# Eight weight rests of an encoder's second MLP: an adding transfer in place of a VectorE subtraction

## The chip, the cores and the metric

The kernel runs on one core of a Trainium2 chip. The metric is the device time of one execution in microseconds (us); the median over runs is compared. Engines are named as the profile names them: PE is the matrix engine (PEld its weight loads), DVE is VectorE, ACT is ScalarE, POOL is GpSimd, SP is SyncE, which issues most of the DMA transfers. SBUF is the on-chip memory with 128 partitions, PSUM the accumulator memory of PE.

## The reference

An encoder of two layers over 256 tokens of width 1024, all in float32. The first half of a layer is a token mixer (pooling, dilated attention, gates). The change lies in the second half, the gated MLP:

```python
def _conv_ffn(xn, w_up, conv_w, conv_b, w_down):
    a, gval = jnp.split(xn @ w_up, 2, axis=-1)
    a = lax.conv_general_dilated(a, ...) + conv_b
    return (jax.nn.gelu(a) * gval) @ w_down

for layer in range(DEPTH):
    h = h + _token_mixer(_rmsnorm(h, norm1[layer]), ...)
    h = h + _conv_ffn(_rmsnorm(h, norm2[layer]), w_up[layer], ...)
return _rmsnorm(h, norm_f)
```

Here w_up is 1024 x 5632 and w_down 2816 x 1024 for each layer.

## The kernel before, in words

**Two parts of every number.** PE multiplies in the type float32r, which keeps fewer bits than float32. So every operand stands as a sum of two parts: the first part is the value rounded to float32r, the rest is what rounding took away. A product is then made of three matmuls: first x first, first x rest, rest x first. For weights, ScalarE makes the first part (the tile wh, a cast, line 191) and VectorE the rest (the tile wl, the loaded weights minus the first part, line 192). Both lines stand in `Weights.open_next`.

**Loads and pieces.** The class `Weights` (line 87) holds the whole program of weight loads in order. SyncE brings 1 MB at a time into one of three buffers (`RAW = 3`, tile raw, line 126), so that each load reuses the buffer of the third load before it. A load holds two pieces, each [128 partitions, 2, 512]; a piece is cast and subtracted into one of five pairs of buffers (`BUFS = 5`, tiles wh and wl). `get` hands out the next piece and prepares pieces ahead: in the MLP's up-projection four of them (`W.LOOK + 1`, line 1485). With five buffers that means: when PE begins with a piece, the buffer of the one before it comes free, and into that goes the piece which is needed four pieces later. `_split` (line 149) first issues the loads that have become due, then the cast and the subtraction.

**The up-projection.** The order of the MLP's work is written out in `ORDER` (line 40): "a0 g0 v0 a1 g1 a2 g2 a3 g3 a4 g4 r5 d0 d1 d2 d3 d4". An "a" or "g" is a sum of 256 rows x 512 columns of the activated branch or of the gate, "r5" the rest of both, "d" parts of the down-projection; v0 belongs to the first layer only. A sum takes two loads (the loop over j in lines 303 to 320) and so four pieces. `by_rows` (line 671) gets a piece, makes its 12 matmuls (`v_sum`, line 661: six for each of two halves of the rows, the second of the six being the first that reads the rest), frees the piece, and calls `unit` (line 1452).

**What else goes on.** After a sum VectorE turns its rows out of PSUM in blocks (line 701). After a "g" sum, `cross` (line 684) sends the turned rows of the pair in 16 transfers of 64 KB to their places; four of them are issued by SyncE in each `unit` of the next "a" sum (line 691). They stand in the same in-order queue as the weight loads. From the unit numbers in `TWOS` (line 42) on, `two_up` (line 1384) makes the convolution, gelu and gate of two blocks of channels, in four steps over four units, on ScalarE and VectorE (lines 1392 to 1430).

**The order of instructions.** `keep_order` (line 643) keeps PE, ScalarE and VectorE to the order of the source from the first up-projection to the last down-projection piece. SyncE's and GpSimd's instructions are placed by the scheduler of the framework, each queue being run in order. GpSimd does only small sums for the norms (lines 467 to 472) once the tables have been built at the start.

Of the kernel before, what the change touches and what calls it, by code (L numbers as in the profile page):

```python
# [10 lines left out]
F32 = mybir.dt.float32  # L11
F32R = mybir.dt.float32r
AF = mybir.ActivationFunctionType
ALU = mybir.AluOpType
# [72 lines left out]
class Weights:  # L87
# [8 lines left out]
    def __init__(self, tc, pool, idle):  # L96
        self.tc, self.nc, self.pool, self.idle = tc, tc.nc, pool, idle
        self.loads, self.pieces = [], []
        self.n_loaded, self.n_split, self.n_got = 0, 0, 0
        self.raw, self.split = {}, {}  # L100
        self.live = set()
        self.behind, self.n_behind = (), 0
        self.n_scaled, self.gains = 0, None
        self.due = 0

    def add(self, src, shape, cuts, tag=None):

        n = len(self.loads)
        self.loads.append((src, shape, tag))
        return [(n, cut, c_shape) for cut, c_shape in cuts]  # L110
# [59 lines left out]
    def open_next(self):  # L170


        nc, i = self.nc, self.n_split
        n, cut, shape, slot = self.pieces[i]
        if slot is None:
            self.live.add(i)
            h, l = (
                self.pool.tile([P, *shape], F32R, tag=tag, bufs=self.BUFS, name=f"{tag}{i}")
                for tag in ("wh", "wl")
            )  # L180
        else:
            tag, part, of = (*slot, 0, 1)[:3]
            if part == 0:
                self.shared = self.idle.tile([P, of, 2, *shape], F32R, tag=tag, name=f"{tag}{i}")
            h, l = self.shared[:, part, 0], self.shared[:, part, 1]
        src = cut(self.raw[n])
        self.split[i] = (h, l)
        self.n_split += 1
        if i >= self.n_scaled:
            return [(  # L190
                lambda: nc.scalar.copy(out=h, in_=src),  # L191
                lambda: nc.vector.tensor_sub(out=l, in0=src, in1=h.bitcast(F32)),  # L192
            )]

        def scaled(j):
            k = i // 2 * shape[0] + j
            g = self.gains[:, k : k + 1]
            return (
                lambda: nc.scalar.activation(h[:, j], src[:, j], AF.Copy, scale=g),
                lambda: nc.vector.scalar_tensor_tensor(  # L200
                    out=l[:, j], in0=src[:, j], scalar=g, in1=h[:, j].bitcast(F32),
                    op0=ALU.mult, op1=ALU.subtract,
                ),
            )

        return [scaled(j) for j in range(shape[0])]
# [15 lines left out]
def encoder(ctx, tc, x, w_in, w_pool, pool_scale, w_a, w_b, w_o, norm1, norm2, w_up, conv_w,  # L222
            conv_b, w_down, rel_bias, norm_f, onehot, edges, out):
    nc = tc.nc
# [9 lines left out]
    W = Weights(tc, wpool, big)  # L234

    def cols(w, c0):

        src = w[:, c0 : c0 + 256].rearrange("(k p) c -> p k c", p=P)
        return W.add(
            src, (8, 256), [((lambda t, j=j: t[:, :, j * P : (j + 1) * P]), (8, P)) for j in (0, 1)]  # L240
        )

    def rows(w, r0, n=2, c0=0, width=1024, tag=None, pieces=2):

        src = w[r0 : r0 + n * P, c0 : c0 + width].rearrange("(k p) c -> p k c", p=P)
        h = n // pieces
        return W.add(
            src, (n, width), [((lambda t, j=j: t[:, j * h : (j + 1) * h, :]), (h, width)) for j in range(pieces)],
            tag,
        )  # L250

    for l in range(DEPTH):
        if l == 0:
            slots = (("m2", 0, 2), ("m2", 1, 2), ("ybig",), ("at2",))
            for j in range(2):
                kept = rows(w_in[l], j * 512, 4, C_V, 512)
                more = rows(w_in[l], j * 512, 4, C_V + 512, 512, "k1" if j else None)
                for n in range(2):
                    W.use(kept[n : n + 1], slots[2 * j + n : 2 * j + n + 1])
                    W.use(more[n : n + 1])  # L260
            W.n_scaled = len(W.pieces)
        else:
            W.use(rows(w_in[l], 512, 4, C_V, 512), (("ybig",), ("at2",)))
            for j in range(2):
                W.use(rows(w_in[l], j * 512, 4, C_V + 512, 512))

        def half_of(w, c0, half, n):
            for j in range(n):
                W.use(rows(w, j * 512, 4, c0 + half.start, 512))

        for half in HALVES:
            half_of(w_in[l], 0, half, 2)
        for c0 in (C_Q + 512, C_K + 512, C_Q + 1024, C_K + 1024):
            half_of(w_in[l], c0, HALVES[0], 2)
        for c in PAIRS:
            q = cols(w_in[l], C_Q + c * 256)
            k = cols(w_in[l], C_K + c * 256)
            if c == 0:
                pool = W.add(
                    w_pool[l].rearrange("g (k p) c -> p (g k) c", p=P), (8, 256),  # L280
                    [((lambda t, j=j: t[:, 4 * j : 4 * j + 4, :]), (4, 256)) for j in range(2)],
                )
                q.insert(1, pool[0])
                k.insert(1, pool[1])
            W.use(q + k)
        half_of(w_in[l], C_V + 1024, HALVES[0], 2)

        for half in HALVES:
            half_of(w_in[l], C_GP, half, 2)
        for half in HALVES:  # L290
            half_of(w_a[l], 0, half, 2)
            half_of(w_in[l], C_GA, half, 2)
            half_of(w_b[l], 0, half, 1)
        for c in range(4):
            W.use(rows(w_o[l], c * 256))
        slots = (("v1",), ("ybig",), ("at2",))
        for kind, n in ORDER.split():
            n = int(n)
            if kind == "v":
                if l + 1 < DEPTH:  # L300
                    W.use(rows(w_in[l + 1], 0, 4, C_V, 512), (("m2", 0, 2), ("m2", 1, 2)))
                continue
            for j in range(2):
                if kind == "d":
                    W.use(rows(w_down[l], (4 * n + 2 * j) * P))
                elif kind == "r":
                    src = w_up[l][j * 512 : (j + 1) * 512].rearrange("(k p) c -> p k c", p=P)
                    c0 = (4 * n * P, 4 * n * P + DFF)
                    W.use(
                        W.add(  # L310
                            tuple(src[:, :, c : c + 256] for c in c0), (4, 2, 256),
                            [
                                ((lambda t, j=j: t[:, 2 * j : 2 * j + 2].rearrange("p k h c -> p k (h c)")), (2, 512))
                                for j in (0, 1)
                            ],
                        )
                    )
                else:
                    p = rows(w_up[l], j * 512, 4, (kind == "g") * DFF + 4 * n * P, 512)
                    W.use(p, slots[2 * j : 2 * j + 2] if (kind, n) == ("a", 0) else ())  # L320
        W.use(rows(w_down[l], (NF - 2) * P))


    h = const.tile([P, 2, D], F32, name="h")
# [214 lines left out]
    def proj(x2):  # L539

        i, (wh, wl) = W.get()
        flush()
        ps = mmp.tile([P, 2, S], F32, tag="mm", name="proj_ps")
        two_sums(ps, lambda k: wh[:, k, :], lambda k: wl[:, k, :], x2, KD)
        W.free(i)
        return ps[:, 0], ps[:, 1]

    def halves(a):

        return a.rearrange("p (t m) -> p t m", t=2)  # L550
# [352 lines left out]
    for l in range(DEPTH):  # L903
# [296 lines left out]
        for c in PAIRS:  # L1200
            for n in range(4):
                src, rest = (halves(a) for a in proj(x2))
# [115 lines left out]
        def begin_mlp():  # L1318
# [12 lines left out]
            out=way[:, 0].rearrange("p j c r -> p c j r"),  # L1331
            in_=th[0][:, 1].rearrange("p (c j r) -> p c j r", c=4, j=4),
# [4 lines left out]
        for j in range(4):  # L1337
            nc.sync.dma_start(
                out=way[32 * j : 32 * j + 32, 1].rearrange("x i c r -> x i (c r)"), in_=blocks_of[j]
# [125 lines left out]
        for kind, n in ORDER.split():  # L1465
# [20 lines left out]
            n = int(n)  # L1486
# [39 lines left out]
```

## Time and profile before

| what | value |
|---|---|
| median of 3 runs (lowest, highest) | 857.34 us (857.09, 857.48) |
| profiled execution: span | 856.1 us |
| second layer's up-projection in it, g0 to r5 | 681.1 to 789.9 us |
| its subtractions for the rests on DVE, whole kernel (line 192) | 278 subtractions, 336.9 us busy |
| its casts on ACT, whole kernel (line 191) | 278 casts, 288.9 us busy |
| mean granted clock of PE | 0.999 |

The profile is one execution. A row of the view by groups gives the line, the engine, what is written and read, the shape, how many, then busy time and the mean of one, then how long the engine was idle just before such instructions and what ended that idling. A row of the timeline gives start and length in us from the span's start. A DMA row gives the queue that issued it (SPq for SyncE's, POOLq for GpSimd's), how many, their size and the median time from issue to landing. Idle time of an engine that does not set the end costs nothing.

### The profile page before, as it was taken

The numbers are of one execution on the slowest core, as the hardware profiler recorded it, in microseconds if no ns is written. First come the engines' busy times: TensorE is split into PE (matmuls) and PEld (weight loads), VectorE is DVE, ScalarE is ACT, GpSimd is POOL, SyncE is SP. The second block draws the span as 40 slices with busy tenths as digits, with TensorE's granted clock in tenths as the row PEclk, the third lists the DMA queues.
The fourth block names the chain that finished last, engine by engine and source line by source line (L and its number), as shares of the span: only waits on it lengthen the run. The fifth ranks groups of instructions, "written<-read, shape, count | busy, mean of one in ns | idle before, by whom it ended". The sixth has DMA issues, their size and how long they took to land.

```text
span 856.1 us, 11279 instructions
## 1 busy us (share of the span) xinstructions
PE 849.1 (99%) x4030; PEld 713.0 (83%) x4030; DVE 648.8 (76%) x918; ACT 476.9 (56%) x700; POOL 19.9 (2%) x53
## 2 busy tenths in 40 slices
PE   9999999999999999999999999999999999999997
PEld 7888888888888888888888889888888888888886
DVE  6967898566767788999656597986568658999874
ACT  7735475444545566767444445654445436766762
POOL 1120000000010000000000000000000000000001
PEclk9999999999999999999999999999999999999999
DMA  8787684764947777777626676758559376777751
GB/s 313 243 256 247 190 278 149 220 231 127 315 173 233 225 236 241 249 232 257 220 99 210 226 233 192 237 162 247 199 200 310 112 228 190 244 242 242 255 181 50
DMA packets 101340, 186.07 MB, mean 217 GB/s; under 512 B 9806, under 2 KB 28702, under 8 KB 101284
## 3 DMA queue, kind: packets, MB, share of 16 engines
q1 hardware_dynamic: 100484, 183.62, 64.9%
q0 software_dynamic: 496, 1.33, 0.5%
q8 instruction: 32, 0.52, 0.3%
q10 hardware_dynamic: 304, 0.40, 0.1%
q14 instruction: 24, 0.20, 0.1%
HBM read 160.65 MB, written 1.59 MB: 190 GB/s over the span
## 4 chain that ended last, share of the span: by engine, by line
PE 99%; POOLq 0%; DVE 0%; ACT 0%; issue 0%; DVEq 0%; POOL 0%; ACTq 0%
PE rows_ps L666 61%; PE res_ps L563 6%; PE res_ps L565 6%; PE res_ps L564 6%; PE v_ps L666 5%; PE proj_ps L535 3%; PE v_ps L788 3%; PE proj_ps L537 2%; PE s_ps L1076 1%; PE o_ps L1151 1%; PE s_ps L1071 1%; PE o_ps L1147 1%; PE xt_ps L494 1%; PE pool_ps L529 0%; PE pool_ps L527 0%; PE pool_ps L528 0%
## 5 line engine op out<-in xcount | busy, mean ns | idle before, releaser
L192 DVE TENSOR_TENSOR wl<-raw,wh 128x1024 fp32r<-128x1024 f32 x278 | 336.9, 1218 | 145.4 <-ACT wh L191 141.6
L666 PE MATMUL rows_ps<-wh,x 128*128 128x512 f32 x1344 | 420.1, 391 | 0.0
L191 ACT CAST wh<-raw 128x1024 fp32r<-128x1024 f32 x278 | 288.9, 1049 | 212.7 <-PE rows_ps L666 131.0
L666 PEld LDWEIGHTS rows_ps<-wh,x 128*128 128x128 f32 x1344 | 252.4, 188 | 52.2
L666 PE MATMUL rows_ps<-wl,x 128*128 128x512 f32 x672 | 261.6, 389 | 0.0
L666 PEld LDWEIGHTS rows_ps<-wl,x 128*128 128x128 f32 x672 | 126.2, 188 | 25.6
L563 PE MATMUL res_ps<-wh,actq 128*128 128x512 f32 (+1 forms) x152 | 57.5, 378 | 0.0
L564 PE MATMUL res_ps<-wl,actq 128*128 128x512 f32 (+1 forms) x152 | 57.4, 378 | 0.0
L565 PE MATMUL res_ps<-wh,actk 128*128 128x512 f32 (+1 forms) x152 | 57.4, 378 | 0.0
L666 PE MATMUL rows_ps<-wh,po 128*128 128x512 f32 x128 | 41.2, 393 | 0.0
L564 PEld LDWEIGHTS res_ps<-wl,actq 128*128 128x128 f32 x152 | 28.6, 188 | 5.4
L563 PEld LDWEIGHTS res_ps<-wh,actq 128*128 128x128 f32 x152 | 28.6, 188 | 5.4
L565 PEld LDWEIGHTS res_ps<-wh,actk 128*128 128x128 f32 x152 | 28.6, 188 | 5.3
L535 PE MATMUL proj_ps<-x,wh 128*128 128x512 f32 x128 | 32.2, 393 | 0.0
L701 DVE STREAM_TRANSPOSE up_rows<-rows_ps 128x512 f32<-128x512 f32 x40 | 26.3, 693 | 3.1 <-PE rows_ps L666 3.1
L666 PEld LDWEIGHTS rows_ps<-wh,po 128*128 128x128 f32 x128 | 24.0, 188 | 4.9
L1393 ACT ACTIVATE yg<-a,prm 128x256 f32<-128x256 f32 x44 | 26.5, 602 | 1.4
L563 PE MATMUL res_ps<-wh,m 128*128 128x512 f32 (+1 forms) x72 | 26.7, 371 | 0.0
L535 PEld LDWEIGHTS proj_ps<-x,wh 128*128 128x128 f32 x128 | 23.1, 189 | 4.2
L565 PE MATMUL res_ps<-wh,m 128*128 128x512 f32 (+1 forms) x72 | 26.4, 366 | 0.0
L564 PE MATMUL res_ps<-wl,m 128*128 128x512 f32 (+1 forms) x72 | 26.4, 366 | 0.0
L463 ACT ACTIVATE junk<-h 128x512 f32<-128x512 f32 (+1 forms) x19 | 10.5, 552 | 27.5 <-DVE h L461 27.5
(225 smaller groups left out, 1051.6 us busy)
## 6 DMA issues: line engine op xcount, KB each, us to landing
raw<-in_w_in_dram SPq DMA_DIRECT2D x56, 1024.0 KB, 5.5
raw<-in_w_up_dram SPq DMA_DIRECT2D x40, 1024.0 KB, 6.0
raw<-in_w_down_dram SPq DMA_DIRECT2D x22, 1024.0 KB, 5.8
up_turned<-up_rows SPq DMA_DIRECT2D x160, 64.0 KB, 3.9
raw<-in_w_a_dram SPq DMA_DIRECT2D x8, 1024.0 KB, 5.0
raw<-in_w_o_dram SPq DMA_DIRECT2D x8, 1024.0 KB, 5.1
qk<-qk_rows SPq DMA_DIRECT2D x64, 64.0 KB, 2.7
pt<-rows SPq DMA_DIRECT2D x64, 64.0 KB, 3.6
```

The costliest lines, as they stand in the source:

```text
L191: lambda: nc.scalar.copy(out=h, in_=src),
L192: lambda: nc.vector.tensor_sub(out=l, in0=src, in1=h.bitcast(F32)),
L463: nc.scalar.activation(junk, new, AF.Square, scale=D**-0.5, accum_out=ss[:, n : n + 1])
L535: nc.tensor.matmul(ps, wh(k), x2[:, k], start=(k == 0), stop=False)
L537: nc.tensor.matmul(ps[:, 1], wl(k), x2[:, k, 0], start=False, stop=(k == nk - 1))
L563: nc.tensor.matmul(ps, ah, wh, start=first, stop=False)
L564: nc.tensor.matmul(ps, ah, wl, start=False, stop=False)
L565: nc.tensor.matmul(ps, al, wh, start=False, stop=last)
L666: nc.tensor.matmul(ps, x2[:, 2 * n + j, part, t, :], w[:, j, :], start=(n + m == 0), stop=(n == of - 1 and m == 5),)
L701: nc.vector.transpose(out=out[:, :, t].rearrange("p j c r -> p c j r"), in_=ps[t].rearrange("p (c j r) -> p c j r", c=4, j=4),)
L788: return nc.tensor.matmul(ps[g][t], a[:, k, t, :], w[:, k % 2, :], start=k == 0 and kind == "hh", stop=k == KD - 1 and kind == "hl",)
L1393: nc.scalar.activation(y, aj, AF.Identity, bias=b, scale=w1)
```

## The change

In the second layer, for the sums a1 to a4 and g1 to g4 (not a0 and g0), the second piece of the second load is marked: one piece in four, eight in all. For a marked piece ScalarE makes the first part as before and then writes its negative into the tile of the rest; a transfer from GpSimd's queue then adds the loaded weights to that tile. VectorE has nothing to do for it. The result is the same sum, the loaded weights minus the first part.

```diff
@@ class Weights, __init__
         self.due = 0
+        self.summed = set()
@@ open_next
         src = cut(self.raw[n])
         self.split[i] = (h, l)
         self.n_split += 1
+        if i in self.summed:
+            return [(
+                lambda: nc.scalar.copy(out=h, in_=src),
+                lambda: nc.scalar.mul(out=l, in_=h.bitcast(F32), mul=-1.0),
+                lambda: nc.gpsimd.dma_start(out=l, in_=src, accum_op=ALU.add),
+            )]
         if i >= self.n_scaled:
             return [(
                 lambda: nc.scalar.copy(out=h, in_=src),
@@ encoder, the loop over ORDER
                     p = rows(w_up[l], j * 512, 4, (kind == "g") * DFF + 4 * n * P, 512)
+                    if l and j and n:
+                        W.summed.add(len(W.pieces) + 1)
                     W.use(p, slots[2 * j : 2 * j + 2] if (kind, n) == ("a", 0) else ())
```

## Prediction

> **What bounds the kernel now.** I read the busy time of the page first, then what the matrix engine waits for, then the stage of the change by itself.
>
> ```profile
> PE 849.1 (99%) x4030; PEld 713.0 (83%) x4030; DVE 648.8 (76%) x918; ACT 476.9 (56%) x700; POOL 19.9 (2%) x53
> ...
> PE gain_ps L377 <- DVE mhalf L366: 1.0, 1, 1.0
> ...
> 681.10:789.90 108.80, 108.80 (x481) 90.10 (x481) 89.80 (x126) 67.76 (x93) 0.00 (x0) 1.00 0.72 236
> 789.90:856.10 66.20, 60.22 (x278) 50.18 (x277) 47.12 (x70) 36.02 (x57) 2.16 (x7) 0.98 0.46 160
> ...
> 681.09 108.80 PE rows_ps L666 x480
> ```
>
> The second line is all that the view of waits has for PE: one wait of 1.0 us in the whole span. The next two are the view by stretches: length, then the busy time of PE, weight loads, DVE, ACT and POOL, the granted clock, the DMA share, GB/s. From 681.1 to 789.9 us, the up-projection of the second layer, PE is busy for all of its 108.80 us at a granted clock of 1.00. The last line, from the chain of waits, says that this is the path: 480 matmuls back to back, 0.2267 us each, so 12 matmuls or 2.72 us for a weight piece, four pieces or 10.88 us for a sum. VectorE's 89.80 us lie beside that. So VectorE's work here ends no wait of PE; the only question is whether the pieces still arrive in time.
>
> How they arrive now:
>
> ```profile
> L192 DVE TENSOR_TENSOR wl<-raw,wh 128x1024 fp32r<-128x1024 f32 x32 | 38.9, 1214 | 16.0 <-ACT wh L191 14.5 <-DMA up_turned<-up_rows 1.5
> L191 ACT CAST wh<-raw 128x1024 fp32r<-128x1024 f32 x33 | 34.6, 1049 | 25.9 <-PE rows_ps L666 18.3 <-DMA raw<-in_w_up_dram 7.5
> L1427 ACT ACTIVATE actq<-yg 128x512 fp32r<-128x512 f32 x6 | 3.8, 630 | 2.1 <-DVE yg L1419 2.1
> ...
> 689.28 1.05 ACT L191 CAST wh<-raw 128x1024 fp32r<-128x1024 f32 x1 [1.67 <-PE rows_ps L666]
> 690.37 1.22 DVE L192 TENSOR_TENSOR wl<-raw,wh 128x1024 fp32r<-128x1024 f32 x1 [1.50 <-ACT wh L191]
> 755.05 1.03 ACT L191 CAST wh<-raw 128x1024 fp32r<-128x1024 f32 x1
> ...
> 843.20 0.22 POOL L467 TENSOR_SCALAR ss<-ss 128x1 f32<-128x1 f32 x1 [171.95 <-ACT junk L463]
> ```
>
> The first three rows are groups of the stretch from 690 to 780 us (busy us, mean ns, idle before), the others single instructions, the last of them GpSimd's first one after the stage. The cast of a piece starts when PE lets go of the buffer of the piece five before it, and that piece is used four pieces later. The cast at 689.28 is that of the first piece the change touches (a1's fourth); the sum g0 begins at 681.09, seven pieces ahead of it, so PE comes to it at 681.09 + 7 x 2.72 = 700.13, and to its rest one matmul later, at 700.36. Its rest is there at 690.37 + 1.22 = 691.59, 8.8 us early. The cast of a4's fourth piece, at 755.05, is the latest against its use, which comes at 765.64 with the rest: 10.6 us, where the first has 11.1.
>
> **The change part by part.** *VectorE.* Eight subtractions leave, 8 x 1.214 = 9.7 us of VectorE's time. What hides them already is PE's 108.80 us, so the gain on the path is nothing.
>
> *ScalarE.* Eight negations come, 1024 elements each from SBUF to SBUF. There is no such row; the cast of the same shape takes 1.05 us, and twice the 512-element multiplication of L1427 takes 1.26. I take 1.06 us, since the cast is the same shape. They are 8.5 us beside ACT's 67.76 of 108.80. Where ACT only casts, each falls into the 1.67 us that ACT waits for PE before the next cast. Where activations follow (after the last six), it moves the next cast by up to 1.1 us, and plain pieces are 8.8 us early. So zero, as long as pieces are early by more than a microsecond.
>
> *GpSimd.* Its queue waits for each negation. The stretch has no GpSimd work at all (0.00 in its column), and the norm's sums start at 843.20, over 50 us after the stage, so nothing waits behind it on that queue.
>
> *The transfer* is the open cost. It carries 512 KB from one SBUF tile into another, adds, and its landing releases both PE (for the rest) and SyncE (for the buffer of the loaded weights). The trace has no adding transfer. Its nearest rows:
>
> ```profile
> fd<-fsb POOLq DMA_DIRECT2D x2, 4.0 KB, 4.0
> bt<-fd POOLq DMA_DIRECT2D x5, 256.0 KB, 5.7
> DMA to landing us min/median/max: 5.1/5.7/6.7
> ...
> raw<-in_w_up_dram SPq DMA_DIRECT2D x12, 1024.0 KB, 6.3
> up_turned<-up_rows SPq DMA_DIRECT2D x64, 64.0 KB, 3.8
> ```
>
> The last number of a row is the median time from issue to landing; the third line gives the spread of the five bt transfers, the last two are of the stretch from 690 to 780 us. A transfer from GpSimd's queue takes 4.0 us when it carries next to nothing. Bytes cost, by SyncE's rows, 6.3 - 3.8 = 2.5 us for 960 KB more, so 1.3 us for 512 KB. To add, the engines must fetch the old values as well, 1 MB in all, hence about 2.6 us. Ends: 4.0 + 1.3 = 5.3 us if the second operand is free. By GpSimd's own rows 252 KB cost 1.7 us, so 1 MB costs 6.9: 10.9 us. I take 4.0 + 2.6 = 6.6, and 0.2 more because the DMA engines are already 0.72 busy in this stage and some of the transfers will share with a load: A = 6.8 us, an estimate. It sits nearer to SyncE's rows because they are the same long runs in this very stage, while the bt rows are five transfers on their way at once.
>
> The Trainium skill ("DMA: Bandwidth & Descriptors", section "Anatomy of one DMA — SWDGE (gpsimd) path") gives for such a transfer about 2.0 us plus bytes over 436 GB/s, an estimate of 3.2 us for 512 KB, with which nothing below would be late and the time would stay at 857.3. The rows do not agree: by that rule 256 KB would take 2.6 us where bt shows 5.7, and 4 KB 2.0 where fd shows 4.0.
>
> *First deadline: the rest itself.* From the start of the cast: 1.05 cast, 1.06 negation, about 0.1 for the two hand-overs, 2.2 us, then A. There are 11.1 us (10.6 for the latest), so by itself this holds until A = 8.9 (8.4). At 6.8 it has 2.1 us left.
>
> *Second deadline: the buffer of the loaded weights.* This is the tight one. There are three such buffers: each load reuses that of the third load before it, and SyncE waits at that load with the row transfers of the up-projection queued behind it.
>
> ```profile
> 691.62 0.37 SPq L126 DMA_DIRECT2D raw<-in_w_up_dram  x1
> 692.85 7.51 SPq L691 DMA_DIRECT2D up_turned<-up_rows  x12
> 700.46 1.00 SPq L126 DMA_DIRECT2D raw<-in_w_up_dram  x1
> ...
> 718.95 0.53 SPq L126 DMA_DIRECT2D raw<-in_w_up_dram  x1
> 719.52 5.80 SPq L691 DMA_DIRECT2D up_turned<-up_rows  x8
> 725.42 0.54 SPq L126 DMA_DIRECT2D raw<-in_w_up_dram  x1
> ...
> ACT wh L191 <- DMA raw<-in_w_up_dram: 7.5, 5, 2.5
> ```
>
> The load at 691.62 starts the moment a1's fourth subtraction is over (691.59); it brings the first two pieces of a2. The load at 700.46, or 725.42 in the next round, brings the last two, and between them SyncE issues 12 or 8 row transfers. The last row (ACT's waits from 690 to 780 us) says that loads come late even now, 7.5 us of ACT's waiting in five places, without harm because pieces are 8.8 us early.
>
> With the change there is a loop from a_n's fourth piece to a_(n+1)'s. The transfer lands; SyncE issues the first load, eight row transfers and the second load: 725.42 - 718.95 = 6.5 us; that load lands 6.3 later; ACT casts the third and fourth piece, 2.1, and negates, 1.06; hand-overs 0.2; then A. In sum 16.2 + A. The loop must fit two sums, 21.76 us, so it holds until A = 5.6. At 6.8 it is 1.2 us too long each time. It runs three times (a1 to a2, a3, a4), and what it eats first is the reserve of 8.9 - A. The loss is 3(A - 5.6) - (8.9 - A) = 4A - 25.7. For A = 6.8 that is 1.5 us. If the order of SyncE's queue stays as in the rows of 691.62 to 700.46, the first time 12 transfers stand between and 4 x 0.63 = 2.5 us are added (7.51 over 12 gives the 0.63): 4.0 us. If the load is put behind the first four, since its buffer comes free later than their rows do, 1.5. I cannot see which, so the middle: 2.8 us.
>
> The first load of a round being late costs nothing by itself: its pieces are used 10.9 us after their casts are due. Behind a g sum's transfer the next two loads follow each other with no row transfers between, so that loop is some 5 us shorter (8 x 0.63) and does not bind.
>
> *Sum.* -0 (VectorE) + 0 (ScalarE, GpSimd) + 2.8 (late pieces) = 2.8 us. A stall here moves everything behind it, because PE has no wait left in which to recover it. The profiled execution has a span of 856.1; the runs' median is 857.34, 1.2 us more, which I take as the part outside the span and leave alone: 857.34 + 2.8 = 860.1 us.
>
> **The rivals.**
>
> *The transfer stays hidden.* For: the fastest bt transfer took 5.1 us, and at A below 6.4 (load behind the first four) or 5.8 (ahead of them) the formula gives no loss; while SyncE stands at the awaited load, few other bytes move. Against: 512 KB with an addition is more than any row of GpSimd's queue. Time 857.3, and no more than 1.7 us above it up to A = 6.85 or 6.2. The skill's rule above leads here too. So does a change that does not do what it says, which I hardly believe: the marked numbers are those of the second piece of each second load, a1 to g4, and eight of them exist.
>
> *The addition is slow.* Where A passes 8.9 the first deadline falls too, in the a and g sums alike; at the upper end of 10.9 the formula gives 17.9 to 20.4 us, about 875 to 878. For: GpSimd's own price per byte. Against: SyncE's price per byte in the same stage.
>
> *Faster.* VectorE's 9.7 us would have to come back in the tail behind the last matmul, 60 us after the stage; the one wait of PE lies at the start of the span. I see no mechanism for 1.7 us.
>
> **How the numbers follow.** About 0.2%, 1.7 us, is what can be told from no change. Slower through late pieces, A between about 6.2 and 8.7: 0.43, with 860.1 as the time. Hidden, or lost by less than 1.7: 0.42. A slow addition: 0.12, ending above 869. Faster: 0.03. So slower 0.55, same 0.42, faster 0.03. The range goes from 856.8, half a microsecond under the median for the hidden case, to the loss at A = 8.7, 9.1 to 11.6 us, so 868.9; it leaves out the slow addition and part of the faster case. For the forecast alone it would be 859.0 to 868.9.
>
> **What would show it.** Eight negations of about 1.06 us on ACT and eight transfers on GpSimd's queue, each landing about 6.8 us after its issue: that number decides. The load of a2's first pieces should issue near 698.3, not 691.6 (691.5 + 6.8). PE should show waits in the second layer's up-projection, the first in a3 or a4, on the landing of these transfers and not on ACT or VectorE, a few microseconds in all. Landings under 6 us with no wait of PE would make the hidden case right; waits already in a1, or at g pieces, would mean that the addition itself is slow. A PE wait anywhere else, or one on a plain piece, would make the working wrong.

## The result, and the profile after

The changed kernel takes 865.07 us (median of 3 runs, 864.78 to 866.01) against 857.34 before: 7.7 us slower, a ratio of 1.0091 (95% interval 1.0073 to 1.0109). The profiled execution has a span of 863.0 us where before it was 856.1, so it shows 6.9 us of the loss.

First the changed kernel's page: its engines, and its DMA queues (packets, MB, share of 16 engines' span). (Nine lines were added above the loops, so lines shift: 192 becomes 199 and 191 becomes 198 for plain pieces, 192 to 194 are the marked ones, 666 becomes 675, 701 becomes 710.)

```profile
PE 851.3 (99%) x4030; PEld 713.3 (83%) x4030; DVE 640.5 (74%) x910; ACT 485.5 (56%) x708; POOL 27.0 (3%) x61
...
q1 hardware_dynamic: 100484, 183.62, 63.6%
q0 software_dynamic: 1648, 5.53, 3.2%
```

Then its view of waits: for PE, what it waited for, with the sum, the count and the longest in us.

```profile
PE rows_ps L675 <- DMA wl<-raw: 4.0, 3, 2.3
PE gain_ps L386 <- DVE mhalf L375: 1.0, 1, 1.0
PE res_ps L573 <- DVE wl L199: 0.5, 1, 0.5
```

VectorE is busy 8.3 us less, ScalarE 8.6 us more, as the change says. The wait for mhalf lies at the kernel's start and was there before. PE now waits three times for a landing of the new transfers, 4.0 us in all, and once more, in the down-projection, for a plain rest from VectorE. The view by stretches adds a third item:

```profile
768.00:770.60 2.60, 0.98 (x4) 0.85 (x5) 2.60 (x5) 1.30 (x3) 0.00 (x0) 1.00 0.42 91
770.60:774.00 3.40, 3.40 (x9) 2.64 (x9) 3.37 (x6) 2.44 (x4) 0.00 (x0) 0.51 0.64 163
```

After the longest wait, 2.3 us, PE's granted clock is 0.51 for 3.4 us: about 1.7 us more. Waits of 4.5 and the slow stretch of 1.7 make 6.2 of the 6.9 us. Another 0.2 is a wait for a load at the kernel's start; the remaining 0.5 was not traced to a place.

The negations as a group of the view by lines (busy time, then ns of one):

```profile
L193 ACT ACTIVATE wl<-wh 128x1024 fp32r<-128x1024 f32 x8 | 8.5, 1061 | 0.3
```

The new transfers' time from issue to landing, and the DMA issues of 690 to 800 us by kind, whose last column is the median landing:

```profile
DMA to landing us min/median/max: 4.4/5.0/5.7
```

```profile
raw<-in_w_up_dram SPq DMA_DIRECT2D x12, 1024.0 KB, 8.9
up_turned<-up_rows SPq DMA_DIRECT2D x74, 64.0 KB, 4.5
wl<-raw POOLq DMA_DIRECT2D x8, 512.0 KB, 5.0
```

The negation costs 1.06 us, as forecast. The transfer lands after 5.0 us, sooner than the forecast 6.8. The loads, of which the prediction took 6.3 us, show 8.9 here. Neither median says much: each time the trace has a landing for only two of the twelve loads, and these are loads of g sums (after, those issued at 708.35 and 757.84). The loads that decide are the second ones of the a sums and of r5; a round is called here the time from one of them to the next, two sums. Their lateness is seen at the cast of the third piece of such a sum, the first to use its second load. For a3, a4 and r5 before, and then for a2, a3, a4 and r5 in the changed kernel:

```profile
731.39 1.05 ACT L191 CAST wh<-raw 128x1024 fp32r<-128x1024 f32 x1 [1.73 <-DMA raw<-in_w_up_dram]
753.56 1.05 ACT L191 CAST wh<-raw 128x1024 fp32r<-128x1024 f32 x1 [2.14 <-DMA raw<-in_w_up_dram]
775.74 1.05 ACT L191 CAST wh<-raw 128x1024 fp32r<-128x1024 f32 x1 [2.54 <-DMA raw<-in_w_up_dram]
```

```profile
711.23 1.05 ACT L198 CAST wh<-raw 128x1024 fp32r<-128x1024 f32 x1 [5.18 <-DMA raw<-in_w_up_dram]
736.11 1.05 ACT L198 CAST wh<-raw 128x1024 fp32r<-128x1024 f32 x1 [4.16 <-DMA raw<-in_w_up_dram]
760.84 1.05 ACT L198 CAST wh<-raw 128x1024 fp32r<-128x1024 f32 x1 [3.50 <-DMA raw<-in_w_up_dram]
786.34 1.05 ACT L198 CAST wh<-raw 128x1024 fp32r<-128x1024 f32 x1 [4.28 <-DMA raw<-in_w_up_dram]
```

Read the distances. PE needs 21.76 us for two sums. Before, the second loads came 22.17 and 22.18 us apart: already a little longer than that, which the 8.8 us of reserve hid. Now they come 24.88, 24.73 and 25.50 us apart. A kernel whose PE did not wait once in this stage held a round that was slower than PE, and the change made it 2.6 to 3.3 us slower.

### The profile page after: what moved, and what is told of

It reads as the page before. It is cut to its first block, busy times and chain, and to the rows that moved or that the text cites. A ratio compares the mean times of both kernels' runs of the same rounds, so it can differ in the third digit from the quotient of the medians.

```text
span 863.0 us, 11314 instructions
## 1 busy us (share of the span) xinstructions
PE 851.3 (99%) x4030; PEld 713.3 (83%) x4030; DVE 640.5 (74%) x910; ACT 485.5 (56%) x708; POOL 27.0 (3%) x61
## 3 DMA queue, kind: packets, MB, share of 16 engines
q1 hardware_dynamic: 100484, 183.62, 63.6%
## 4 chain that ended last, share of the span: by engine, by line
PE 85%; DMA 5%; DVE 4%; ACT 2%; issue 2%; SPq 1%; POOLq 0%; DVEq 0%; ACTq 0%; POOL 0%
PE rows_ps L675 50%; PE res_ps L573 6%; PE res_ps L574 6%; PE res_ps L572 6%; PE v_ps L675 5%; DMA raw<-in_w_up_dram 3%; PE proj_ps L544 3%; PE v_ps L797 2%; PE proj_ps L546 2%; DVE wl L199 1%; PE s_ps L1085 1%; PE o_ps L1160 1%; DVE yg L1403 1%; DMA wl<-raw 1%; PE s_ps L1080 1%
## 5 line engine op out<-in xcount | busy, mean ns | idle before, releaser
L199 DVE TENSOR_TENSOR wl<-raw,wh 128x1024 fp32r<-128x1024 f32 x270 | 327.1, 1217 | 150.3 <-ACT wh L198 147.7
L198 ACT CAST wh<-raw 128x1024 fp32r<-128x1024 f32 x270 | 280.5, 1049 | 207.0 <-PE rows_ps L675 112.4
L1403 DVE SCALAR_TENSOR_TENSOR yg<-a,prm,yg 128x255 f32<-128x255 f32 x44 | 21.1, 480 | 13.2 <-ACT yg L1402 13.2
L572 PE MATMUL res_ps<-wh,m 128*128 128x512 f32 (+1 forms) x72 | 26.7, 371 | 0.0
```

The lines of the kernel that those rows point to most:

```text
L572: nc.tensor.matmul(ps, ah, wh, start=first, stop=False)
L1403: nc.vector.scalar_tensor_tensor(out=y[:, 1:], in0=aj[:, : S - 1], scalar=w0, in1=y[:, 1:], op0=ALU.mult, op1=ALU.add)
```

## The experiments

All ratios are against the kernel before on the same chip, with 95% intervals.

**neg_only.** ScalarE's part alone:

```diff
-                lambda: nc.gpsimd.dma_start(out=l, in_=src, accum_op=ALU.add),
+                lambda: nc.vector.tensor_add(out=l, in0=src, in1=l.bitcast(F32)),
```

> ScalarE's part of the change alone: the eight negations stay, VectorE adds the loaded weights to the negative, no transfer. Loop theory (the transfer holds the buffer of the loaded weights, the loads behind it come late): no loss, 857.3 within 1.0. Rival, the eight negations of 1.06 us push the casts and the activations back: most of the 7.7 us remain, 862 to 865.

857.56 us, ratio 1.0003 (0.9993 to 1.0012). The negations are not the cause.

**a_only** and **g_only.** Half of the marks each:

```diff
-                    if l and j and n:
+                    if l and j and n and kind == "a":    # g_only: "g"
```

> Only the four a pieces are marked, the g pieces get VectorE's subtraction. Loop theory: the second load of a round no longer shares the DMA engines with a g transfer and lands after about 6.0 us as before, not 8.3; the loop is then 4.8 + 1 + 6.45 + 6.0 + 3.7 = 22.0, three times 0.2 us too long, far below the reserve of 4.1: 857.3 to 858. Rival, the a pieces' own lateness is enough (two of the three waits of PE are at a pieces): 862 or more. Rival, the bytes alone: half the loss, about 861.

> Only the four g pieces are marked. Loop theory: nothing holds the buffer of an a sum, no loop, no loss, 857.3 to 858, though the second load of each round still shares with the g transfer and lands after about 8 us. Rival, the bytes alone: half the loss, about 861. Rival, a rest that comes from a transfer is late by itself: 859 to 861.

a_only: 857.63 us, ratio 1.0000 (0.9990 to 1.0009). g_only: 862.71 us, ratio 1.0057 (1.0041 to 1.0074), so 5.1 us lost. The first was as the loop theory had it, the second lies above every time expected: by the prediction the a pieces carry the loop and the g pieces do not bind. It is the other way round. PE's waits, first of a_only, then of g_only:

```profile
PE gain_ps L386 <- DVE mhalf L375: 1.0, 1, 1.0
PE v_ps L797 <- ACT wh L206: 0.4, 1, 0.4
```

```profile
PE rows_ps L675 <- DMA wl<-raw: 4.2, 2, 2.7
PE gain_ps L386 <- DVE mhalf L375: 1.0, 1, 1.0
PE res_ps L573 <- DVE wl L199: 0.7, 2, 0.4
```

Their casts of the third pieces of a3, a4 and r5, in the same order:

```profile
732.17 1.05 ACT L198 CAST wh<-raw 128x1024 fp32r<-128x1024 f32 x1 [2.16 <-DMA raw<-in_w_up_dram]
755.24 1.05 ACT L198 CAST wh<-raw 128x1024 fp32r<-128x1024 f32 x1 [2.75 <-DMA raw<-in_w_up_dram]
778.16 1.05 ACT L198 CAST wh<-raw 128x1024 fp32r<-128x1024 f32 x1 [2.61 <-DMA raw<-in_w_up_dram]
```

```profile
736.86 1.05 ACT L198 CAST wh<-raw 128x1024 fp32r<-128x1024 f32 x1 [5.90 <-DMA raw<-in_w_up_dram]
761.27 1.05 ACT L198 CAST wh<-raw 128x1024 fp32r<-128x1024 f32 x1 [3.83 <-DMA raw<-in_w_up_dram]
786.08 1.05 ACT L198 CAST wh<-raw 128x1024 fp32r<-128x1024 f32 x1 [4.22 <-DMA raw<-in_w_up_dram]
```

The rounds are 23.07 and 22.92 us in a_only, 24.41 and 24.81 in g_only, against 22.17 and 22.18 before. So the a transfers are not without effect: they lengthen a round too, by less than 1 us where the g ones add 2.2 to 2.6, and the reserve hides it. Why they do was not traced. On top of the g transfers they may well cost something: the changed kernel's ratio is 1.0091, g_only's 1.0057, with intervals that barely overlap.

**own_buffer.** All eight transfers, but the second load of each marked a sum goes into a tile that is free in this stage, outside the ring of three:

```diff
-                    p = rows(w_up[l], j * 512, 4, (kind == "g") * DFF + 4 * n * P, 512)
+                    own = "m2" if l and j and n and kind == "a" else None
+                    p = rows(w_up[l], j * 512, 4, (kind == "g") * DFF + 4 * n * P, 512, own)
```

> All eight transfers stay, but the second load of each marked a sum goes into a tile of its own that is free in this stage, so the ring of three buffers is never held by an a transfer. Loop theory: the loop is cut, 857.3 to 858.5. Rivals, the bytes or the rest's own latency or the negations: as the changed kernel, 864 to 866.

864.46 us, ratio 1.0080 (1.0065 to 1.0095). The loop that the prediction described, through the buffer held by an a transfer, is cut here and the loss stays. That theory fell. The changed kernel's trace shows why. The first load of a2, behind a1's transfer, was held until 696.24. But from the next round on SyncE stands at the row transfers ahead of such a load and not at the load: a2's transfer landed at 719.27, and the load into its buffer came up only at 721.03, behind four row transfers. SyncE's two largest waits from 690 to 780 us before, and then its wait for rows and its wait for the new transfers in the changed kernel:

```profile
SPq L691 <- DVE up_rows L701: 25.1, 4, 8.3
SPq L126 <- DVE wl L192: 10.3, 5, 5.0
```

```profile
SPq L700 <- DVE up_rows L710: 35.8, 4, 10.1
SPq L127 <- DMA wl<-raw: 1.2, 2, 0.7
```

What was left: the g transfers' bytes, the buffer that they hold, or PE's wait on their landing. The next four runs tell these apart.

**g_bytes.** VectorE makes the g rests again; the negation and the transfer stay, but the transfer adds the first part into a tile that nobody reads:

```diff
+            scr = self.idle.tile([P, *shape], F32R, tag="m2", name=f"scr{i}")
             return [(
                 lambda: nc.scalar.copy(out=h, in_=src),
-                lambda: nc.scalar.mul(out=l, in_=h.bitcast(F32), mul=-1.0),
-                lambda: nc.gpsimd.dma_start(out=l, in_=src, accum_op=ALU.add),
+                lambda: nc.scalar.mul(out=scr, in_=h.bitcast(F32), mul=-1.0),
+                lambda: nc.gpsimd.dma_start(out=scr, in_=h.bitcast(F32), accum_op=ALU.add),
+                lambda: nc.vector.tensor_sub(out=l, in0=src, in1=h.bitcast(F32)),
             )]
```

> The four g pieces get VectorE's subtraction again; negation and transfer stay, but the transfer adds the first part (not the loaded weights) into a tile that nobody reads, so its bytes move at the same time and it holds no buffer of loaded weights. If holding the buffer is the cause (the next two loads start together after the landing and run into the third): 857.3 to 858.3. If the bytes are the cause: as g_only, 862 to 863.

863.15 us, ratio 1.0067 (1.0052 to 1.0082): as slow as g_only, though no buffer of loaded weights is held and no piece waits for a landing. Casts and subtractions do not become slower either: from 681 to 800 us a plain cast takes 1044 ns (1047 before), a plain subtraction 1213 (1214). That leaves the transfers' bytes on the DMA engines. The casts of the third pieces, and PE's waits:

```profile
735.16 1.05 ACT L200 CAST wh<-raw 128x1024 fp32r<-128x1024 f32 x1 [4.80 <-DMA raw<-in_w_up_dram]
759.69 1.05 ACT L200 CAST wh<-raw 128x1024 fp32r<-128x1024 f32 x1 [3.95 <-DMA raw<-in_w_up_dram]
784.50 1.04 ACT L200 CAST wh<-raw 128x1024 fp32r<-128x1024 f32 x1 [4.23 <-DMA raw<-in_w_up_dram]
```

```profile
PE rows_ps L677 <- ACT wh L200: 1.0, 1, 1.0
PE res_ps L575 <- DVE wl L201: 0.8, 1, 0.8
PE rows_ps L677 <- DVE wl L201: 0.8, 1, 0.8
PE res_ps L574 <- ACT wh L200: 0.5, 1, 0.5
```

The casts are 24.53 and 24.81 us apart, as in g_only. PE waits later and for plain pieces, because the loads behind them are late.

**g_hold.** As g_bytes, with the loaded weights as the source (`in_=src`), so that the buffer is held as well:

> The four g pieces get VectorE's subtraction for PE; negation and transfer stay and the transfer adds the loaded weights into a tile that nobody reads, so the buffer is held as in g_only and only PE's wait on the landing is gone. If late loads alone stop PE: as g_only, 862 to 863. If it takes the late loads and the transfer's own 5 us on top: the reserve grows from 4 to 8.8 us, against a loop that is some 8 us too long over three rounds, so 857.5 to 859.5.

863.10 us, ratio 1.0065 (1.0047 to 1.0083). Holding the buffer adds nothing that can be told from g_bytes. This came out as the first branch says, late loads alone stop PE.

**g_dram.** As g_only, but added straight from HBM:

```diff
-                lambda: nc.gpsimd.dma_start(out=l, in_=src, accum_op=ALU.add),
+                lambda: nc.gpsimd.dma_start(out=l, in_=cut(self.loads[n][0]), accum_op=ALU.add),
```

> The four g pieces as in g_only, but the transfer adds the weights straight from HBM, so that the buffer of loaded weights is free after ScalarE's cast; PE still waits for the landing, and the bytes are the same (512 KB of them read from HBM). If holding the buffer is the cause: 857.3 to 858.3. If the bytes or the rest's own latency are: 861 to 863.

863.73 us, ratio 1.0072 (1.0056 to 1.0088), 0.7 us above the second branch and against the buffer theory. Here the transfers themselves come late; PE's wait for them, and their landings:

```profile
PE rows_ps L675 <- DMA wl<-in_w_up_dram: 3.4, 3, 1.8
```

```profile
DMA to landing us min/median/max: 7.8/9.4/10.3
```

The longest landing, 10.3 us, makes PE wait the longest, 1.8: so a rest may land 8.5 us after its issue before PE waits. This is the prediction's first deadline (8.9 by its arithmetic), measured.

**first_piece.** All eight transfers at the first piece of the second load:

```diff
-                        W.summed.add(len(W.pieces) + 1)
+                        W.summed.add(len(W.pieces))
```

> All eight transfers, but at the first piece of the second load and not at its second. The transfer starts 2.72 us earlier against the end of the load's use, so it holds the buffer 2 to 5 us past VectorE's last read and not 5 to 8. If the hold is the cause, most of the loss goes: 857.5 to 860. If the bytes are: 863 to 866 as the changed kernel.

864.69 us, ratio 1.0086 (1.0069 to 1.0103): the branch of the bytes.

So the bytes of the g transfers are the cause of the greater part of the loss. Why the g ones? In the changed kernel, GpSimd issues g2's transfer at 725.72 and it lands at 731.24; SyncE's queue around it:

```profile
707.87 0.92 SPq L127 DMA_DIRECT2D raw<-in_w_up_dram  x2
718.51 2.41 SPq L700 DMA_DIRECT2D up_turned<-up_rows  x4
721.03 0.52 SPq L127 DMA_DIRECT2D raw<-in_w_up_dram  x1
721.60 5.74 SPq L700 DMA_DIRECT2D up_turned<-up_rows  x8
727.43 1.33 SPq L127 DMA_DIRECT2D raw<-in_w_up_dram  x1
```

The second load of a3 is issued at 727.43, in the middle of the g transfer, and lands at 736.04, 8.6 us later (the kernel before: issued at 725.42, landed at 731.31, 5.9). In a_only the same load takes 5.7 us, from 726.39 to 732.09. An a transfer, such as that from 714.62 to 719.27, falls into the pause in which SyncE waits for the next turned rows; what it can still meet there are loads of g sums, whose pieces no cast waits for in the changed kernel. The page gives the size: the software queue's share grew from 0.5% of 856.1 us to 3.2% of 863.0, by 23.3 us of all 16 engines for eight transfers, 2.9 us each. A megabyte of loads takes 63.6% of 863.0 over 183.62, 3.0 us. By these shares an adding transfer of half a megabyte loads the engines like a plain one of a whole.

Two runs tested that lateness is carried from round to round until the reserve is gone.

**g1_g2.** Only g1 and g2 marked (`n in (1, 2) and kind == "g"`):

> Only the pieces of g1 and g2 are marked. New theory, lateness is carried from round to round and stops PE only when the reserve is gone: two transfers, some 2.5 to 5 us, do not use it up, 857.3 to 858.3. Rival, each transfer costs its share of the 5.1 us of g_only: 859.5 to 860.5.

858.40 us, ratio 1.0016 (1.0007 to 1.0026): 0.9 us, a fifth of g_only's loss for half of its transfers, slightly above the expected. Single executions lie between 857.31 and 861.37 us, and the profiled one, 857.75, lost next to nothing, so its trace shows the rounds but no wait of PE. Its casts, after the last transfer, return to the old distance, 21.99 and 22.14 us, so the round is longer only where a transfer falls into it:

```profile
734.12 1.05 ACT L198 CAST wh<-raw 128x1024 fp32r<-128x1024 f32 x1 [3.46 <-DMA raw<-in_w_up_dram]
756.11 1.05 ACT L198 CAST wh<-raw 128x1024 fp32r<-128x1024 f32 x1 [2.35 <-DMA raw<-in_w_up_dram]
778.25 1.05 ACT L198 CAST wh<-raw 128x1024 fp32r<-128x1024 f32 x1 [2.50 <-DMA raw<-in_w_up_dram]
```

**g_half_bytes.** As g_bytes with half of each transfer (`out=scr[:, :1], in_=h[:, :1].bitcast(F32)`):

> As g_bytes (VectorE makes the rests, the transfer ends in a tile that nobody reads), with half the bytes in each of the four transfers. New theory, carried lateness against a reserve of 8.8 us: the second load lands some 1.5 us later per round and not 3, so at most 858.5. Rival, each byte costs the same: half of the 5.8 us of g_bytes, 859.8 to 860.7.

858.68 us, ratio 1.0013 (1.0004 to 1.0022): about a fifth of the loss of g_bytes for half of the bytes, 0.2 us above the theory's bound and 1.1 below the rival's. The loss is not proportional to bytes. Nor is it the number of packets: GpSimd's queue has 1072 on the pages of both runs.

Two runs tried to cut the loop, with all eight transfers left in.

**rows_on_act.** ScalarE's queue issues the row transfers of this stage, so that no load stands behind them:

```diff
-                nc.sync.dma_start(out=out[b, i], in_=in_[a, j])
+                (nc.scalar if rows_on_act else nc.sync).dma_start(out=out[b, i], in_=in_[a, j])
```

(`rows_on_act` is set for the second layer's up-projection alone.)

> The changed kernel with all eight transfers, but the row transfers of the second layer's up-projection are issued from ScalarE's queue, so no weight load stands behind them. New theory, a loop of load, casts, activations, turned rows, row transfers, load, which is as long as a round already and grows by what the g transfer takes from the second load: the loop is cut, 857.3 to 859. Rival, the DMA engines as such carry too much in this stage: 863 to 866.

888.44 us, ratio 1.0358 (1.0342 to 1.0373), far worse than either theory. ScalarE itself stops now; among its waits from 681 to 830 us stand

```profile
ACT y L1423 <- issue: 15.4, 3, 7.3
ACT y L1417 <- issue: 10.7, 3, 3.8
```

26 us in front of the activations that follow the transfers in its order. The edit put a new bound in place of the old one and says nothing about the loop.

**loads_earlier.** Each load stands one place earlier in SyncE's order from this stage on:

```diff
-            self.due = n + self.RAW
+            self.due = n + self.RAW + (self.early is not None and i >= self.early)
```

(`self.early` is the piece with which the second layer's stage begins, plus eight.)

> The changed kernel with all eight transfers, but from the second layer's up-projection on each load stands one place earlier in SyncE's order, so that the second load of a round has four row transfers ahead of it and not twelve and a load. New theory: the loop is shorter by some 5 us, 857.3 to 859. Rival, the DMA engines as such: 863 to 866. Rival, SyncE waits for a buffer with rows behind it and the rows come late: 860 or more.

876.95 us, ratio 1.0221 (1.0185 to 1.0257). The last rival happened: rows come late because SyncE waits for a buffer ahead of them (37.6 us at loads for the new transfers' landings, from 681 to 820 us), and ScalarE waits for rows:

```profile
ACT a L1404 <- DMA up_turned<-up_rows: 21.1, 5, 5.7
```

Neither run settles by which links the round closes. From the traces it reads: second load, casts, activations, the turning of the g rows behind them on VectorE, their transfers, the loads behind those. That reading is argued, not shown. Shown are the round's length and that the g transfers' bytes lengthen it. That PE stops when the reserve is used up fits g1_g2 and g_half_bytes, where half of the transfers, or of the bytes, cost about a fifth of the loss, though both came out 0.1 to 0.2 us above the bounds set for it.

## Why the prediction was right and wrong

The direction and the range held (860.1 forecast, 856.8 to 868.9, measured 865.07). The loss was 7.7 us where 2.8 was forecast, and the mechanism under that number was the wrong one. That the time still fell into the range was luck.

- *No gain on the path, no recovery.* Right: with VectorE's 8.3 us less nothing was gained, and what PE lost in this stage stayed lost.
- *Negations.* Right in size, 1.06 us, and free (neg_only).
- *The transfer, A = 6.8 us.* It was 5.0 (4.4 to 5.7), below the lower end of 5.3. The term for the bytes, 2.6, is near the 2.9 that the queue's share gives; then about 2 us are left for the start, where 4.0 were taken from transfers of 4 KB. That split is a subtraction and was not measured. The Trainium skill's formula ("DMA: Bandwidth & Descriptors", "Anatomy of one DMA — SWDGE (gpsimd) path") gives an estimate of 3.2 us; measured is 5.0, so it is too short here, too.
- *First deadline.* Right: 8.9 reckoned, 8.5 measured in g_dram; at 5.0 it does not bind by itself.
- *Second deadline: the step that failed.* "The transfer lands; SyncE issues the first load": that the a transfers close the loop by holding a buffer. With A = 5.0 the formula 4A - 25.7 gives no loss at all; a_only lost nothing, own_buffer cut that loop and kept the loss. SyncE waited 1.2 us in all for the new transfers' landings and 35.8 for turned rows; the prediction had it wait at the load. The sentence that a g sum's transfer "does not bind" was wrong outright: g_only lost 5.1 us.
- *What stood in its place.* The 6.3 us for a load's landing was taken as fixed (the load that decides took 5.9 us for a3 before), and sharing got 0.2 us, in A. The g transfer falls onto that load, which then took 8.6 us. The round came to 24.7 to 25.5 us, where the prediction had 23.0 with other parts.
- *What could have been read before.* The casts at 731.39, 753.56 and 775.74 were in the trace: 22.2 us apart where PE needs 21.76. The prediction quoted the sum of these waits (7.5 us in five places) and not that they grew, 1.73, 2.14, 2.54. Waits that grow from round to round meant here that the rounds were already too long for PE.
- *The signs named.* PE's first wait did come in a3 and on a landing. The first load of a2 was issued at 696.24, not 698.3, behind four row transfers, the branch without the 2.5 us. Waits at g pieces were to mean a slow addition; one came in g3, with additions that were fast. A wait on a plain piece was to make the working wrong; one of 0.5 us came, in the down-projection.

## What to carry to other kernels

Before extra bytes are put on the DMA engines of a kernel whose matrix engine never waits, measure the distance of successive late loads against what the matrix engine needs for the same work: if the waits for them grow from round to round, the reserve is being spent, and a transfer that falls on the deciding load spends it faster. Here it mattered where in the round a transfer falls: four lengthened the round by less than 1 us and cost nothing, four others lengthened it by 2.2 to 2.6 us and cost 5. In this kernel an adding transfer had to be counted with twice its bytes.

## What was not expected of the hardware

PE's granted clock fell to 0.51 for 3.4 us after a wait of 2.3 us, which made the wait dearer by 1.7 us. It does not follow every such wait; in g_only, after one of 2.7 us (1.7 in the first of these rows, 1.0 in the second), the clock stayed at 1.00:

```profile
776.00:780.00 4.00, 2.30 (x11) 1.57 (x9) 3.62 (x7) 3.48 (x6) 0.48 (x1) 1.00 1.07 227
780.00:782.00 2.00, 0.97 (x4) 0.83 (x5) 2.00 (x3) 0.85 (x2) 0.00 (x0) 1.00 0.73 212
782.00:786.00 4.00, 4.00 (x20) 3.27 (x19) 1.68 (x4) 0.00 (x0) 0.00 (x0) 1.00 0.95 317
```

The Trainium skill ("TensorE: Matmul & The Clock Gate", Part 1 on the clock gate) says that the clock is halved after at least one idle window of about 3.4 us. Here 2.3 us were enough once and 2.7 us not another time, so the length of a single wait does not decide it. In g_bytes it was 0.57 from 787 to 791 us, after waits of 1.0 and 0.8 us. The same part of the Trainium skill calls its window free-running, by which the moment of the wait would count as well; that was not tried.
